# Strided attention: the output products as eight full-array matmuls with a block matrix of weights, the weights turned as 32-bit words, and a store with a nearer wait

## The chip, the cores and the metric

The kernel runs on one core of a Trainium2 chip. Its five engines are TensorE (PE, with PEld for its weight loads), VectorE (DVE), ScalarE (ACT), GpSimd (POOL) and SyncE (SP), which here only issues DMA transfers. The metric is the device time of one execution in microseconds (us). Beside it stands the span of the profiled execution, which is counted from the first to the last event in the trace and is some 1.9 us shorter than that execution's own time.

## The reference

Q, K and V have the shape (8 batches, 12 heads, 1024 positions, 64 dims) in 32-bit floats. Every query attends to 16 keys only, those at positions 0, 64, 128, ... 960:

```python
attend_positions = np.arange(0, seq, stride)          # 16 positions, stride 64
scores = np.einsum('bhqd,bhkd->bhqk', q, k) * scale   # scale = 1/8
weights = np.exp(scores - np.max(scores, axis=-1, keepdims=True))
weights = weights / (np.sum(weights, axis=-1, keepdims=True) + 1e-10)
result[:, :, i, :] = np.einsum('bhqk,bhkd->bhqd', weights, v)[:, :, 0, :]
```

So 96 heads of 1024 x 64 are read and 96 heads of 1024 x 64 are written: 25.2 MB in, 25.2 MB out, and little arithmetic for each byte.

## The kernel before

**Tiling.** The 96 heads are taken as 24 groups (`NG`) of 4 heads. A group is 1 MiB of Q: 128 partitions of 2048 floats. Sixteen groups have a place each in one big buffer, `big`; the outputs of a group overwrite its Q there, and are stored from there. Groups 16 to 23 reuse the first eight places, so their loads wait for the stores of groups 0 to 7.

**One group** runs through these steps, in the names of the code:

1. `cast_a` on ACT and `cast_p` on POOL turn the two halves of Q into bfloat16 (`qb`).
2. `turn` on DVE transposes 32 x 32 blocks of `qb`, as 32-bit words (pairs of bfloat16), into `qt`.
3. `score_products` on PE: scores into PSUM (`sc`).
4. `lay` on DVE transposes the scores into `s_t`; `highest` on DVE takes the maximum over 16 keys (`top`).
5. `subtract` on POOL takes the maximum away (`diff`), `raise_` on ACT takes the exponential (`ex`), `sums` and `inverse` on DVE add up and invert (`total`, `rec`).
6. `normalise` on POOL multiplies `ex` by `rec` into the weights `w_n`, in bfloat16.
7. `back` on DVE transposes `w_n` in 32 x 32 blocks of single bfloat16 values into `w_t`.
8. `output_products` on PE: for each half of the outputs (`h` = 0, 1) eight matmuls, four for each of two 64 x 64 corners of the array, into `o`.
9. `evict` on ACT copies each half from PSUM into `big`.
10. `store` on SP sends the group, or from group 10 on two groups at once (2 MiB), to the output.

`place_k` and `place_v` on POOL bring the keys and values of the next groups into `k_cur` and `v_cur`.

**Order.** The order of the steps is written out by hand. A loop over `n` puts at place n the steps of several groups (`spread(n)`, `turn_over(n + 1)`, `add_up(n - 1)`, `weights_back(n - 2)`, `evict(n - 3, 1)` and so on); each engine runs its own steps in that order. DVE and PE run groups 2 to 21 in hardware loops, `dve_stream` with four groups a round and `pe_stream` with two. SP issues its transfers strictly in order, so a transfer that waits holds up those behind it.

**Waits.** `Program` records every step with what it reads and writes and plans the waits. A step raises either the semaphore of its engine or a named counter, a "gate", which the hardware loops count (`ev` is the gate of evictions; PE waits on it before it overwrites `o`). A step whose signal is a gate cannot be waited for through its engine's semaphore. So where another engine needs such a step, the planner lets it wait for the next step behind it on the same engine that has no gate:

```python
while d is not None and self.ops[d]["gate"]:
    later = (j for j in range(d + 1, i) if self.ops[j]["lane"] == p["lane"])
    d = next(later, None)
```

All evictions carry the gate `ev` except those of the last group, 23. The store of groups 20 and 21 needs the evictions of group 21. The next step on ACT without a gate is the first eviction of group 23, and the store waits for that.

The store of groups 22 and 23, the last, is issued behind a barrier of all engines.

Of the kernel before, what the change touches and what calls it, by code (L numbers as in the profile page):

```python
# [174 lines left out]
def kernel(  # L175
# [38 lines left out]
    s_t = [sb.tile([P, 32, NK], FP32, name=f"s_t{i}") for i in range(2)]  # L214
    diff = [sb.tile([P, 32, NK], FP32, name=f"diff{i}") for i in range(2)]
# [58 lines left out]
    def constants():  # L274
# [14 lines left out]
        for i in range(2):  # L289
            op("DVE", lambda i=i: nc.vector.memset(ex[i], EPS), writes=[f"ex{i}"])  # L290
        op("DVE", lambda: nc.vector.tensor_reduce(
            out=s_sel,
# [73 lines left out]

    def place(to, from_, g, n, needs, writes, gate):
        dims = "pgabx"[: len(to.shape)]
        flat = f"{' '.join(dims)} -> p ({' '.join(dims[1:])})"
        op("POOL", lambda: nc.gpsimd.tensor_copy(  # L370
            out=to[:, g % 2 : g % 2 + n].rearrange(flat).bitcast(I32),
            in_=from_[:, g : g + n].rearrange(flat).bitcast(I32),
        ), reads=needs, writes=writes, gate=None if g == 1 else gate)

    def place_k(g):
        n = 1 if g < 2 else 2
        place(k_cur, k_all, g, n,
              ["k_zero"] + [f"k{i % 2}{s}" for i in range(g, g + n) for s in range(4)],
              [f"k_cur{i % 2}" for i in range(g, g + n)], "stK")

    def place_v(g):
        n = 1 if g < 2 else 2
        place(v_cur, v_all, g, n,
              [f"v_all{i % 2}{x}" for i in range(g, g + n) for x in range(4)],
              [f"v_cur{i % 2}" for i in range(g, g + n)], "stV")

# [18 lines left out]
    def subtract(g):  # L405
        op("POOL", lambda: nc.gpsimd.tensor_tensor(  # L406
            out=diff[g % 2], in0=s_t[g % 2],
            in1=top[g % 2].unsqueeze(2).to_broadcast([P, 32, NK]), op=ALU.subtract,
        ), reads=[f"s_t{g % 2}", f"top{g % 2}"], writes=[f"diff{g % 2}"])

    def raise_(g):
        op("ACT", lambda: nc.scalar.activation(  # L412
            out=ex[g % 2][:, :, 0:NK], in_=diff[g % 2], func=AF.Exp, bias=0.0, scale=scale,
        ), reads=[f"diff{g % 2}"], writes=[f"ex{g % 2}"], gate="ex" if g < LAST - 1 else None)

# [14 lines left out]
    def normalise(g):  # L430
        op("POOL", lambda: nc.gpsimd.tensor_tensor(  # L431
            out=w_n[g % 2], in0=ex[g % 2][:, :, 0:NK],
            in1=rec[g % 2].unsqueeze(2).to_broadcast([P, 32, NK]), op=ALU.mult,
        ), reads=[f"ex{g % 2}", f"rec{g % 2}"], writes=[f"w_n{g % 2}"], gate="wn")

    def back(g):
        return nc.vector.transpose(  # L437
            _ap_with(w_t[g % 2], [w_t[g % 2].ap[0], [64, 8], [1, 2], [2, 32]]),
            w_n[g % 2].rearrange("p n k -> p (n k)"),
        )  # L440

# [8 lines left out]
    def evict(g, h):  # L450
        o = o_ps[h].rearrange("p c (t x d) -> p x (c t) d", t=2, d=D)
        to = big[:, g % NB].rearrange("p (x t d) -> p x t d", x=4, t=8)[:, :, 4 * h : 4 * h + 4]
        op("ACT", lambda: nc.scalar.copy(to, o), reads=[f"o{h}"], writes=[f"b{g % NB}{'ab'[h]}"],  # L453
           gate=None if g == NG - 1 else "ev")

# [37 lines left out]
    def on(f, g, *a, **how):  # L493
        if 0 <= g < NG:
            f(g, *a, **how)
# [53 lines left out]
    def pe_stream(sems, gates):  # L549
# [17 lines left out]
        def output_products(g, h):  # L567
            for t in range(4):
                for b in range(2):
                    half_b = slice(64 * b, 64 * b + 64)  # L570
                    r = pe.matmul(  # L571
                        o_ps[h][half_b, t // 2, 256 * (t % 2) : 256 * (t % 2) + 256],
                        lhsT=w_t[g % 2][half_b, 4 * h + t],
                        rhs=v_cur[half_b, g % 2].rearrange("p x d -> p (x d)"),
                        start=True, stop=True, tile_position=(64 * b, 64 * b),
                    )
            r.then_inc(sems["PE"], 1)
# [88 lines left out]
```

## Time and profile before

| | |
|---|---|
| median of 3 runs | 128.7 us (128.56 to 128.8) |
| profiled execution, own time | 128.46 us |
| its span | 126.6 us |
| busy: PE, DVE, ACT, POOL | 64.2, 100.5, 90.2, 84.2 us |
| DMA: moved, mean rate over the span | 51.15 MB, 404 GB/s |

How to read the views that follow. The page gives busy time of each engine as a share of the span. A stage table gives for each stretch of time the busy microseconds of each engine (with the number of instructions that began there), the granted PE clock as a share of the full one, the mean busy share of the 16 DMA engines and the rate that they moved. A timeline row has the start, the duration, the engine, the line and the operation; merged rows have a count (x16). In square brackets stands how long the engine was idle before, and what ended that. A group row has the count, then the total busy time in us and the mean of one instruction in ns. The chain of waits is the work that ended last, followed back step by step; its rows hold what each step added to the chain, which is less than the duration of an instruction where two overlap.

### The profile page before, as it was taken

Reading aid. Unit: us, or ns where it says so; the run is one execution under the profiler, and the core shown is the slowest. Engines: PE = TensorE matmul, PEld = TensorE weight load, DVE = VectorE, ACT = ScalarE, POOL = GpSimd, SP = SyncE. Lnnn points to the kernel's source line nnn. Section 1 sums busy time; section 2 is a strip of 40 time slices with the busy share of each in tenths; the row PEclk is TensorE's granted clock in tenths of the full one; section 3 lists DMA queues with packets and bytes.
Section 4 is the critical chain, followed back from the end, with each engine's and each line's share of the span. In section 5 each row is a group of like instructions: output and inputs, shape, how many; then the busy total and the mean of one; then the engine's idle time right before and its main releaser. Section 6 shows DMA issues by size and latency. Waiting matters only on the chain.

```text
span 126.6 us, 1871 instructions
## 1 busy us (share of the span) xinstructions
PE 64.2 (51%) x604; PEld 32.7 (26%) x604; DVE 100.5 (79%) x159; ACT 90.2 (71%) x106; POOL 84.2 (67%) x110
## 2 busy tenths in 40 slices
PE   0000702338777788777345777779755336970000
PEld 0000100004543245543112543335522213530000
DVE  4329699499999999999999999999999999520000
ACT  4016679557899988989999789998899669692000
POOL 4016742859888898888898888898888867600000
PEclk9999999999999999999999555555589998699555
DMA  3899999999999989999999989989899999988993
GB/s 93 311 405 441 404 466 445 393 445 404 476 435 393 445 362 422 479 399 396 479 386 430 500 352 453 479 349 494 378 430 430 425 430 425 425 347 342 414 414 166
DMA packets 6803, 51.15 MB, mean 404 GB/s; under 512 B 3760, under 2 KB 3760, under 8 KB 3760
## 3 DMA queue, kind: packets, MB, share of 16 engines
q1 hardware_dynamic: 6800, 51.12, 96.5%
q14 instruction: 3, 0.02, 0.1%
HBM read 25.95 MB, written 25.17 MB: 404 GB/s over the span
## 4 chain that ended last, share of the span: by engine, by line
DVE 68%; ACT 6%; DMA 5%; PE 5%; issue 3%; POOL 3%; DVEq 1%; SPq 0%
DVE qt L361 20%; DVE s_t L392 12%; DVE top L399 11%; DVE total L417 11%; DVE w_t L437 9%; DMA big<-in_K_dram 5%; DVE rec L424 3%; ACT big L453 3%; PE sc L557 2%; PE o L571 2%; DVE v_all L339 2%; POOL qb L357 1%; POOL diff L406 1%; ACT k_all L308 1%; ACT qb L352 1%
## 5 line engine op out<-in xcount | busy, mean ns | idle before, releaser
L453 ACT COPY big<-o 128x1024 f32<-128x1024 f32 x48 | 46.2, 1016 | 8.4 <-PE o L571 8.4
L571 PE MATMUL o<-v_cur,w_t 64*64 64x256 bf16 x384 | 38.5, 361 | 21.1 <-DVE w_t L437 18.6
L571 PEld LDWEIGHTS o<-v_cur,w_t 64*64 64x64 bf16 x384 | 28.7, 142 | 40.5 <-ACT big L453 27.2
L557 PE MATMUL sc<-qt,k_cur 128*32 128x512 bf16 x216 | 25.2, 557 | 15.4 <-DVE qt L361 10.0
L431 POOL TENSOR_TENSOR w_n<-ex,rec 128x512 bf16<-128x512 f32 x24 | 25.4, 1057 | 8.9 <-DVE rec L424 8.9
L406 POOL TENSOR_TENSOR diff<-s_t,top 128x512 f32<-128x512 f32 x24 | 25.4, 1058 | 7.9 <-DVE top L399 7.9
L361 DVE STREAM_TRANSPOSE qt<-qb 128x1024 int32<-128x1024 int32 x24 | 28.8, 1202 | 0.0
L352 ACT CAST qb<-big 128x1024 bf16<-128x1024 f32 x24 | 25.2, 1054 | 0.0
L357 POOL CAST qb<-big 128x1024 bf16<-128x1024 f32 x24 | 25.0, 1043 | 0.0
L412 ACT ACTIVATE ex<-diff 128x512 f32<-128x512 f32 x24 | 15.3, 638 | 6.2 <-POOL diff L406 6.1
L437 DVE STREAM_TRANSPOSE w_t<-w_n 128x512 bf16<-128x512 bf16 x24 | 17.9, 746 | 1.6 <-POOL w_n L431 1.5
L392 DVE STREAM_TRANSPOSE s_t<-sc 128x512 f32<-128x512 f32 x24 | 16.1, 671 | 1.6 <-PE sc L557 1.6
L417 DVE TENSOR_REDUCE total<-ex 128x32 f32<-128x544 f32 x24 | 17.0, 707 | 0.3 <-ACT ex L412 0.3
L399 DVE TENSOR_REDUCE top<-s_t 128x32 f32<-128x512 f32 x24 | 15.5, 647 | 0.1
L557 PEld LDWEIGHTS sc<-qt,k_cur 128*32 128x32 bf16 x216 | 3.6, 103 | 26.9 <-DVE qt L361 19.8
L315 PE MATMUL o<-big,perm_v 128*128 128x384 bf16 x4 | 1.5, 520 | 12.8 <-POOL big L323 12.8
L424 DVE RECIPROCAL rec<-total 128x32 f32<-128x32 f32 x24 | 7.4, 308 | 0.0
L370 POOL COPY v_cur<-v_all 128x256 int32<-128x256 int32 (+1 forms) x13 | 5.0, 384 | 1.1 <-PE o L571 1.1
L370 POOL COPY k_cur<-k_all 128x128 int32<-128x128 int32 (+1 forms) x13 | 3.7, 281 | 2.1 <-ACT k_all L308 1.8
L298 ACT CAST big<-big 128x384 bf16<-128x384 f32 x1 | 0.5, 511 | 5.6 <-DMA big<-in_K_dram 5.6
L299 POOL CAST big<-big 128x384 bf16<-128x384 f32 x1 | 0.5, 507 | 5.6 <-DMA big<-in_K_dram 5.6
L301 DVE STREAM_TRANSPOSE big<-big 128x384 int32<-128x384 int32 x1 | 0.6, 579 | 4.3 <-POOL big L299 4.3
(18 smaller groups left out, 18.8 us busy)
## 6 DMA issues: line engine op xcount, KB each, us to landing
big<-in_Q_dram SPq DMA_DIRECT2D x24, 1024.0 KB, 12.2
out_dram<-big SPq DMA_DIRECT2D x7, 2048.0 KB, 13.7
out_dram<-big SPq DMA_DIRECT2D x10, 1024.0 KB, 14.1
big<-in_K_dram SPq DMA_DIRECT2D x1, 384.0 KB, 6.8
big<-in_V_dram SPq DMA_DIRECT2D x1, 384.0 KB, 7.9
```

The lines of the kernel that those rows point to most:

```text
L352: op("ACT", lambda: nc.scalar.copy(b[:, half:], q[:, half:]), reads=[f"b{g % NB}{h}" for h in "ab"], writes=[f"qb{g % 4}1"])
L357: op("POOL", lambda: nc.gpsimd.tensor_copy(out=b[:, 0:half], in_=q[:, 0:half]), reads=[f"b{g % NB}{h}" for h in "ab"] + [f"qb{g % 4}1"] * ...
L361: return nc.vector.transpose(qt[g % 2].bitcast(I32), qb[g % 4].bitcast(I32))
L392: return nc.vector.transpose(s_t[g % 2].rearrange("p n k -> p (n k)"), sc_ps[g % 2])
L399: return nc.vector.tensor_reduce(out=top[g % 2], in_=s_t[g % 2], op=ALU.max, axis=mybir.AxisListType.X)
L406: op("POOL", lambda: nc.gpsimd.tensor_tensor(out=diff[g % 2], in0=s_t[g % 2], in1=top[g % 2].unsqueeze(2).to_broadcast([P, 32, NK]), op=AL ...
L417: return nc.vector.tensor_reduce(out=total[g % 2], in_=ex[g % 2], op=ALU.add, axis=mybir.AxisListType.X)
L431: op("POOL", lambda: nc.gpsimd.tensor_tensor(out=w_n[g % 2], in0=ex[g % 2][:, :, 0:NK], in1=rec[g % 2].unsqueeze(2).to_broadcast([P, 32, N ...
L437: return nc.vector.transpose(_ap_with(w_t[g % 2], [w_t[g % 2].ap[0], [64, 8], [1, 2], [2, 32]]), w_n[g % 2].rearrange("p n k -> p (n k)"),)
L453: op("ACT", lambda: nc.scalar.copy(to, o), reads=[f"o{h}"], writes=[f"b{g % NB}{'ab'[h]}"], gate=None if g == NG - 1 else "ev")
L557: r = pe.matmul(sc_ps[g % 2][32 * c : 32 * c + 32], lhsT=k_cur[:, g % 2, f, b], rhs=_ap_with(qt[g % 2], [qt[g % 2].ap[0], [D, 8], [16 * D, ...
L571: r = pe.matmul(o_ps[h][half_b, t // 2, 256 * (t % 2) : 256 * (t % 2) + 256], lhsT=w_t[g % 2][half_b, 4 * h + t], rhs=v_cur[half_b, g % 2] ...
```

## The change

The weights of a group are now laid out and turned in another way, and the output products are made from a block matrix:

- `normalise` writes `w_n` with two bytes of every four: the weights of two neighbouring groups of queries (x = 0, 1) alternate, so that a pair lies in one 32-bit word. Its reads are as before.
- `back` transposes `w_n` as 32-bit words, in two instructions for 64 partitions each, into the two diagonal 64 x 64 blocks of `w_t`, which is now 128 wide. The other two blocks are set to zero once, by two new `memset` instructions at the start on DVE.
- `output_products` makes four matmuls of 128 x 128 by 256 columns for each half where it made eight of 64 x 64 by 256.
- `subtract` works in place in `s_t`; the tile `diff` is gone, and `raise_` reads `s_t`.
- The second eviction of group 21 has no gate any more. A step that does nothing but wait for it on ACT raises the gate `ev` in its stead. The store of groups 20 and 21 thereby waits for this eviction itself.
- `place_k` and `place_v` are written out separately, and do the same.

```diff
-    w_t = [sb.tile([P, 8, 64], BF16, name=f"w_t{i}") for i in range(2)]
+    w_t = [sb.tile([P, 8, P], BF16, name=f"w_t{i}") for i in range(2)]
...
+        for i in range(2):
+            op("DVE", lambda i=i: nc.vector.memset(w_t[i], 0.0), writes=[f"w_t{i}"])
...
     def subtract(g):
         op("POOL", lambda: nc.gpsimd.tensor_tensor(
-            out=diff[g % 2], in0=s_t[g % 2],
+            out=s_t[g % 2], in0=s_t[g % 2],
             in1=top[g % 2].unsqueeze(2).to_broadcast([P, 32, NK]), op=ALU.subtract,
-        ), reads=[f"s_t{g % 2}", f"top{g % 2}"], writes=[f"diff{g % 2}"])
+        ), reads=[f"s_t{g % 2}", f"top{g % 2}"], writes=[f"s_t{g % 2}"])
...
     def normalise(g):
         op("POOL", lambda: nc.gpsimd.tensor_tensor(
-            out=w_n[g % 2], in0=ex[g % 2][:, :, 0:NK],
-            in1=rec[g % 2].unsqueeze(2).to_broadcast([P, 32, NK]), op=ALU.mult,
+            out=_ap_with(w_n[g % 2], [w_n[g % 2].ap[0], [64, 8], [1, 2], [32, 2], [2, NK]]),
+            in0=ex[g % 2][:, :, 0:NK].rearrange("p (t x u) k -> p t x u k", x=2, u=2),
+            in1=rec[g % 2].rearrange("p (t x u) -> p t x u", x=2, u=2).unsqueeze(4).to_broadcast([P, 8, 2, 2, NK]),
+            op=ALU.mult,
         ), reads=[f"ex{g % 2}", f"rec{g % 2}"], writes=[f"w_n{g % 2}"], gate="wn")
 
     def back(g):
-        return nc.vector.transpose(
-            _ap_with(w_t[g % 2], [w_t[g % 2].ap[0], [64, 8], [1, 2], [2, 32]]),
-            w_n[g % 2].rearrange("p n k -> p (n k)"),
-        )
+        for b in range(2):
+            rows = slice(64 * b, 64 * b + 64)
+            r = nc.vector.transpose(
+                w_t[g % 2][rows, :, rows].bitcast(I32),
+                w_n[g % 2][rows].rearrange("p n k -> p (n k)").bitcast(I32),
+            )
+        return r
...
         op("ACT", lambda: nc.scalar.copy(to, o), reads=[f"o{h}"], writes=[f"b{g % NB}{'ab'[h]}"],
-           gate=None if g == NG - 1 else "ev")
+           gate=None if g == NG - 1 or (g, h) == (NG - 3, 1) else "ev")
...
         on(evict, n - 3, 1)
+        if n - 3 == NG - 3:
+            op("ACT", lambda: nc.scalar.nop(), reads=[f"b{(NG - 3) % NB}b"], gate="ev")
...
         def output_products(g, h):
             for t in range(4):
-                for b in range(2):
-                    half_b = slice(64 * b, 64 * b + 64)
-                    r = pe.matmul(
-                        o_ps[h][half_b, t // 2, 256 * (t % 2) : 256 * (t % 2) + 256],
-                        lhsT=w_t[g % 2][half_b, 4 * h + t],
-                        rhs=v_cur[half_b, g % 2].rearrange("p x d -> p (x d)"),
-                        start=True, stop=True, tile_position=(64 * b, 64 * b),
-                    )
+                r = pe.matmul(
+                    o_ps[h][:, t // 2, 256 * (t % 2) : 256 * (t % 2) + 256],
+                    lhsT=w_t[g % 2][:, 4 * h + t],
+                    rhs=v_cur[:, g % 2].rearrange("p x d -> p (x d)"),
+                    start=True, stop=True,
+                )
             r.then_inc(sems["PE"], 1)
```

Where this shows in the order of the instructions: first DVE, one group in the hardware loop, before. A row holds the line, the operation, what it writes and reads (the number behind a name tells two buffers apart) and the size of its output.

```order
L392 STREAM_TRANSPOSE s_t_73<-sc_92 128x512
L361 STREAM_TRANSPOSE qt_72<-qb_70 128x1024
L399 TENSOR_REDUCE top_83<-s_t_73 128x32
L417 TENSOR_REDUCE total_86<-ex_78 128x32
L437 STREAM_TRANSPOSE w_t_81<-w_n_79 128x8x2x32
L424 RECIPROCAL rec_88<-total_86 128x32
```

The same place now:

```order
L389 STREAM_TRANSPOSE s_t_73<-sc_90 128x512
L362 STREAM_TRANSPOSE qt_72<-qb_70 128x1024
L396 TENSOR_REDUCE top_81<-s_t_73 128x32
L414 TENSOR_REDUCE total_84<-ex_76 128x32
L438 STREAM_TRANSPOSE w_t_79<-w_n_77 64x8x32 x2
L421 RECIPROCAL rec_86<-total_84 128x32
```

One transpose of 512 elements a partition has become two, of 256 32-bit words a partition each, at the same place.

Next the end of ACT's program, with the semaphores each instruction waits for, before. The rows are the exponential of group 22, both evictions of group 20, the exponential of group 23, both evictions of group 21 and the first of group 22.

```order
L412 ACTIVATE ex0_77<-diff0_75 128x32x16 [waits at_POOL]
L453 COPY big_66<-o0_94 128x4x256 [waits at_PE]
L453 COPY big_66<-o1_95 128x4x256 [waits at_PE]
L412 ACTIVATE ex1_78<-diff1_76 128x32x16 [waits at_POOL]
L453 COPY big_66<-o0_94 128x4x256 [waits at_PE]
L453 COPY big_66<-o1_95 128x4x256 [waits at_PE]
L453 COPY big_66<-o0_94 128x4x256 [waits at_PE]
```

And now:

```order
L409 ACTIVATE ex0_75<-s_t0_73 128x32x16 [waits at_POOL]
L455 COPY big_66<-o0_92 128x4x256 [waits at_PE]
L455 COPY big_66<-o1_93 128x4x256 [waits at_PE]
L409 ACTIVATE ex1_76<-s_t1_74 128x32x16 [waits at_POOL]
L455 COPY big_66<-o0_92 128x4x256 [waits at_PE]
L455 COPY big_66<-o1_93 128x4x256 [waits at_PE]
L455 COPY big_66<-o0_92 128x4x256 [waits at_ACT,at_PE]
```

The instructions are the same; ahead of the first eviction of group 22 (the last row) stands the new wait of ACT for its own eviction of group 21. SP's transfers stand in the same order as before.

More of the change, by code (lines that the diff above doesn't have):

```diff
@@ L406, in subtract @@
         op("POOL", lambda: nc.gpsimd.tensor_tensor(
[L407 removed]
+            out=s_t[g % 2], in0=s_t[g % 2],
             in1=top[g % 2].unsqueeze(2).to_broadcast([P, 32, NK]), op=ALU.subtract,
[L409 removed]
+        ), reads=[f"s_t{g % 2}", f"top{g % 2}"], writes=[f"s_t{g % 2}"])
     def raise_(g):
         op("ACT", lambda: nc.scalar.activation(
[L413 to L414 removed]
+            out=ex[g % 2][:, :, 0:NK], in_=s_t[g % 2], func=AF.Exp, bias=0.0, scale=scale,
+        ), reads=[f"s_t{g % 2}"], writes=[f"ex{g % 2}"], gate="ex" if g < LAST - 1 else None)
     def sums(g):
```

24 lines of the change are left out of this document (10 added, 14 removed).

## Prediction

> **What bounds the kernel now.** I read the page first, for the busy shares and the chain.
>
> ```profile
> span 126.6 us, 1871 instructions
> PE 64.2 (51%) x604; PEld 32.7 (26%) x604; DVE 100.5 (79%) x159; ACT 90.2 (71%) x106; POOL 84.2 (67%) x110
> q1 hardware_dynamic: 6800, 51.12, 96.5%
> DVE 68%; ACT 6%; DMA 5%; PE 5%; issue 3%; POOL 3%; DVEq 1%; SPq 0%
> ```
>
> The chain of waits says DVE. The queue of the transfers says something else: its 16 engines were taken for 96.5% of the span. Both can be nearly full, so the question is which of them the end waits for. The stage table answers that; its last two columns are the DMA share and the rate in GB/s.
>
> ```profile
> 26.00:41.00 15.00, 10.48 (x88) 5.62 (x90) 15.00 (x25) 11.75 (x14) 12.08 (x16) 1.00 1.00 430
> 86.00:101.00 15.00, 9.11 (x101) 4.96 (x99) 15.00 (x25) 13.05 (x16) 13.35 (x17) 0.77 1.02 431
> 113.00:113.60 0.60, 0.51 (x8) 0.24 (x6) 0.00 (x0) 0.60 (x1) 0.00 (x0) 1.00 0.65 273
> 113.60:114.80 1.20, 0.00 (x0) 0.00 (x0) 0.00 (x0) 1.07 (x2) 0.00 (x0) 1.00 0.07 27
> 114.80:124.60 9.80, 0.00 (x0) 0.00 (x0) 0.00 (x0) 0.00 (x0) 0.00 (x0) 0.60 1.01 428
> 124.60:126.60 2.00, 0.00 (x0) 0.00 (x0) 0.00 (x0) 0.00 (x0) 0.00 (x0) 0.50 0.00 0
> ```
>
> In the loop DVE is busy for 15.00 of 15 us, and the transfers run at 430 GB/s with a share of 1.0, early and late. The rate is the same 428 GB/s at the end, where no engine works any more. So I take 428 GB/s as what the transfers can do here, and DVE as an engine that merely keeps up: it makes outputs while a backlog of transfers stands ahead of them. The backlog runs out once: from 113.60 to 114.80 the transfers stand still (27 GB/s). Then 4 MiB are left, which take the 9.80 us to 124.60; 2.00 us of closing follow. Why they stand still is seen on the timeline.
>
> ```profile
> 104.92 0.54 SPq L34 DMA_DIRECT2D out_dram<-big  x1
> 108.71 1.93 ACT L453 COPY big<-o 128x1024 f32<-128x1024 f32 x2 [1.02 <-PE o L571]
> 110.91 3.76 ACT L453 COPY big<-o 128x1024 f32<-128x1024 f32 x4 [0.27 <-PE o L571]
> 113.78 0.54 SPq L34 DMA_DIRECT2D out_dram<-big  x1
> 115.04 0.54 SPq L34 DMA_DIRECT2D out_dram<-big  x1
> SPq L34 <- ACT big L453: 8.3, 1, 8.3
> ```
>
> The three transfers are the stores of groups 18+19, 20+21 and 22+23. Group 21 is evicted by 108.71 + 1.93 = 110.64. Its store goes out at 113.78, just after the third of the next four evictions (110.91 + 3 x 0.94 = 113.73), the first of group 23. Its data move from 114.80, 1.0 us after the issue. By then the store of groups 18+19 has been through for 1.2 us.
>
> **The store's wait.** With its wait on the eviction that it needs, the store of groups 20+21 goes out at about 110.7, and could move data from 111.7. The store ahead holds the transfers until 113.6. So there is no gap: the remaining 4 MiB run from 113.6 to 113.6 + 9.8 = 123.4, provided that the last store is there in time. It is issued at 115.04 and could move from 116.0; the store ahead of it needs until 113.6 + 4.9 = 118.5. The gain is the stall of 1.20 us, less the 27/428 of it (0.08 us) that did move something. The slow 0.6 us before it (273 GB/s) may give (1 - 273/428) x 0.6 = 0.22 us more, as a queue that does not run dry has no tailing off. That is **1.1 to 1.35 us, taken as 1.2**. The new step on ACT waits only for ACT's own eviction; behind it stand the evictions of groups 22 and 23. The first of these began 0.27 us after the one before it anyway, for want of PE: this covers the step. If it took more, the last store would be late by the difference, and has 2.5 us to spare.
>
> **The turn on DVE.** The chain's rows give what each step of a group adds, overlap left out:
>
> ```profile
> 58.45 0.66 DVE w_t L437
> 59.12 0.21 DVE rec L424
> 59.32 0.58 DVE s_t L392
> 59.90 1.12 DVE qt L361
> 61.02 0.57 DVE top L399
> 61.59 0.62 DVE total L417
> ```
>
> Together 3.76 us a group. Two transposes of 256 words replace one of 512 values (0.66). No 64-partition transpose is in the trace. From 512 elements (0.58, `s_t`) to 1024 words (1.12, `qt`) an element costs 1.05 ns, and 0.04 us is left as fixed cost: 256 words then take 0.31, two of them 0.62, **0.04 us less** than now. The other end comes from the shortest DVE step, the reciprocal: 32 elements take 0.21, so up to 0.18 us could be fixed. Then two halves take 2 x (0.27 + 0.18) = 0.90, 0.24 us more. I take 0.62, since it comes from the same operation; nothing speaks for less, as both forms pass 512 elements. Over 24 groups that is 1.0 us earlier on DVE, and worth nothing: the transfers are full without it, and the earlier stores would only stand in the queue longer.
>
> **The margin.** How late may the evictions become? The store of groups 20+21 could move from 111.7 and is wanted at 113.6: 1.9 us. Beyond that each microsecond late is one lost, and the gain is gone at 1.9 + 1.2 = 3.1 us. Spread over groups 0 to 21 that is 0.14 us a group, from whichever engine.
>
> **The strided write on POOL.**
>
> ```profile
> L431 POOL TENSOR_TENSOR w_n<-ex,rec 128x512 bf16<-128x512 f32 x24 | 25.4, 1057 | 8.9 <-DVE rec L424 8.9
> L406 POOL TENSOR_TENSOR diff<-s_t,top 128x512 f32<-128x512 f32 x24 | 25.4, 1058 | 7.9 <-DVE top L399 7.9
> L357 POOL CAST qb<-big 128x1024 bf16<-128x1024 f32 x24 | 25.0, 1043 | 0.0
> L370 POOL COPY v_cur<-v_all 128x256 int32<-128x256 int32 x11 | 4.4, 400 | 1.1 <-PE o L571 1.1
> ```
>
> `normalise` and `subtract` take the same 1057 and 1058 ns, though one writes 2 bytes an element and the other 4: the size of the write sets nothing here. No row writes every other 2 bytes. One more pass of the data through POOL would be the upper bound: the one-input rows (1043 for 1024, 400 for 256) give 0.84 ns an element, so 512 elements 0.43 us. POOL is busy for 13.35 of 15 us, so of a group's 3.76 us 0.41 is free. Hence 0 to 0.43 us is taken in, to 0.02 us a group; I take 0, by the two equal rows. `subtract` in place moves as many bytes as before: 0.
>
> The Trainium skill ("GPSIMD Engine Reference", section 7, Performance pitfalls) has a rule that could speak against this: reads whose inner step is over 8 bytes cost about half as much again. It tells of reads; here the new step is 4 bytes and on a write, and the read of `ex` keeps its step. By that rule the sum stays as it is. No row of this trace has such a step on POOL.
>
> **The matmuls.**
>
> ```profile
> 59.22 1.06 PE L571 MATMUL o<-v_cur,w_t 64*64 64x256 bf16 x16 [0.86 <-DVE w_t L437]
> 55.41 1.91 PE L571 MATMUL o<-v_cur,w_t 64*64 64x256 bf16 x16 [0.90 <-DVE w_t L437]
> 12.82 1.46 PE L315 MATMUL o<-big,perm_v 128*128 128x384 bf16 x4 [12.82 <-POOL big L323]
> 59.27 0.64 ACT L412 ACTIVATE ex<-diff 128x512 f32<-128x512 f32 x1
> 61.51 0.70 DVE L417 TENSOR_REDUCE total<-ex 128x32 f32<-128x544 f32 x1
> ```
>
> A group's sixteen 64 x 64 matmuls take 1.06 us, or 1.91 in slow stretches. The only full-array matmuls are four of 384 columns at the start, 1.46 us; eight of 256 columns scale to 1.46 x 2 x 256/384 = 1.95 us as an upper bound, and half of the slow row (0.5 us) is below anything seen. I take the same as now. The ends stay harmless: PE is idle for 30% of the loop or more (10.48 and 9.11 of 15 us are busy), and at worst a group's outputs come 0.9 us later. ACT then evicts later, and its exponential behind that: it ends at 59.91 where DVE wants it at 61.51, 1.6 us to spare. Behind the loop, where PE itself is on the chain, 0.9 us a group for two groups stays below the 1.9 us of margin.
>
> **The two memsets** stand on DVE ahead of the first reduction.
>
> ```profile
> 3.28 1.08 DVE L290 MEMSET ex<- 128x544 f32 x2
> 4.29 0.23 DVE L291 TENSOR_REDUCE s_sel<-identity 128x4 f32<-128x128 bf16 x1
> 8.81 0.58 DVE L301 STREAM_TRANSPOSE big<-big 128x384 int32<-128x384 int32 x1 [4.30 <-POOL big L299]
> ```
>
> Two like them take 1.08 us, and DVE waits 4.30 us there for the keys. Without that cover they would cost those 1.08 us, within the margin.
>
> **The sum** is -1.2 us, all from the store's wait: 128.46 - 1.2 = 127.26 us by the profiled execution, whose own time is 0.24 us below the median shown. Moved to the median it is 127.5. **I predict 127.4 us**; with the 1.1 to 1.35 and the spread of the runs shown, 127.0 to 127.8 is this case's own range.
>
> **The rivals.**
>
> The forecast: the stall goes, all else is covered. 0.73.
>
> More: if 428 GB/s were what the stores happen to offer and not a limit, DVE's 1.0 us would come on top, and the time would be 126.4 us. Against it: the rate is the same with and without work beside it. 0.04.
>
> The stall moves instead of going. Two stores then drain together, and the transfers could fall back to the 273 GB/s seen before the stall at the joint between two stores, or the last store may wait for something late in the barrier ahead of it (its issue at 115.04 already comes 0.37 after the last eviction's end at 114.67). Then the time stays within 0.2% of now (about what runs of this kernel can tell from no change): 128.5 to 128.9 us. Against it speaks that every earlier store follows another without a dip to be seen in the stage rows. 0.09.
>
> Slower, by DVE. If a transpose of 64 partitions pays the reciprocal's fixed cost, a group takes 4.00 us in place of 3.76. DVE is busy without pause, so it all adds up: 22 x 0.24 = 5.3 us at group 21. The store of groups 20+21 then moves from 111.7 + 5.3 = 117.0, and its data and the last end at 126.8, 2.2 us later than the 124.6 now: 130.7 us. It decides from 0.14 us a group, that is, from 0.40 us a half. For it: no row shows this form. Against it: all long steps fit 0.04 us fixed, and the reciprocal may be slow by itself. 0.08.
>
> Slower, by POOL. If the strided write doubles `normalise` to 2.11 us, POOL has 1.06 - 0.41 = 0.65 us a group too little, 14.3 us over 22 groups: data end at 111.7 + 14.3 + 9.8 = 135.8, and the time is 139.7 us. It decides from 0.41 + 0.14 = 0.55 us an instruction, above the extra pass of 0.43. At half as much again (0.53) it is 128.0 us. 0.04 for the slow case, 0.02 for the one between.
>
> **How the numbers follow.** Faster by over 0.2%: the forecast, the case of more and POOL's case between, 0.73 + 0.04 + 0.02 = 0.79. Within it: 0.09. Slower: 0.08 + 0.04 = 0.12. The range from 126.6 to 128.5 holds the forecast, POOL's middle case, half of the case of more and the edge of the no-change case, about 0.8.
>
> **What would show it.** In the changed profile: the store of groups 20+21 issued within 0.2 us of the second eviction of group 21, and no stage between 104 and 122 us with a DMA share far below 1.0; `w_t` at two rows of about 0.31 in the chain; `normalise` at 1.06 us; the span near 125.4. DVE's loop should close some 0.9 us earlier with nothing gained by it. I am wrong if the transfers are not the limit: if an end of DVE 1 us earlier moves the end by as much, or if 428 GB/s is exceeded over a long stretch. I am wrong on the other side if `w_t` or `w_n` is longer than the bounds above.

## The result, and the profile after

| | before | after |
|---|---|---|
| median | 128.62 us (128.52 to 128.8, 5 runs) | 130.78 us (130.63 to 130.97, 5 runs) |
| ratio | | 1.0168, 95% interval 1.0154 to 1.0182 |
| profiled execution, span | 128.46, 126.6 us | 130.88, 129.0 us |
| one group on DVE, in the chain | 3.76 us | 4.07 us |
| second eviction of group 21 ends | 110.64 us | 116.39 us |

The change makes the kernel 2.2 us slower. One run of all is left out of the figures: 160.91 us for the changed kernel with the old wait, whose other three runs took 134.24 to 134.39. First the page of the changed kernel: busy shares and the queue.

```profile
span 129.0 us, 1514 instructions
PE 66.9 (52%) x412; PEld 26.4 (20%) x412; DVE 107.5 (83%) x185; ACT 90.3 (70%) x106; POOL 84.2 (65%) x110
q1 hardware_dynamic: 6800, 51.12, 94.7%
```

DVE is busy 7.0 us longer than before (100.5), and the queue's share has gone down from 96.5 to 94.7%: transfers now wait for something. The chain of waits of the changed kernel shows for what; start, time added and work in each row, one group:

```profile
60.56 0.34 DVE w_t L438
60.90 0.01 issue
60.92 0.44 DVE w_t L438
61.36 0.03 issue
61.39 0.35 DVE rec L421
61.74 0.57 DVE s_t L389
```

From the start of the first half of the turn to the start of `s_t` it is 61.74 - 60.56 = 1.18 us, where turn and reciprocal took 59.32 - 58.45 = 0.87 us before. The 0.31 us are the whole difference between 4.07 and 3.76 us a group. Two things strike: the second half adds 0.44 us, 0.10 more than the first of the same size, and the reciprocal behind it adds 0.35 + 0.03 us, where it added 0.21.

The timeline of the changed kernel at the end:

```profile
110.57 0.54 SPq L34 DMA_DIRECT2D out_dram<-big  x1
114.46 1.93 ACT L455 COPY big<-o 128x1024 f32<-128x1024 f32 x2 [0.82 <-PE o L573]
116.41 0.54 SPq L34 DMA_DIRECT2D out_dram<-big  x1
118.94 1.93 ACT L455 COPY big<-o 128x1024 f32<-128x1024 f32 x2 [0.17 <-PE o L573]
121.04 0.54 SPq L34 DMA_DIRECT2D out_dram<-big  x1
```

The store of groups 20+21 goes out 0.02 us after the eviction that it needs (114.46 + 1.93 = 116.39), as the change intends. But this eviction comes 5.75 us later than before. The stage table of the changed kernel (again the DMA share and GB/s in the last two columns):

```profile
109.60:110.80 1.20, 0.53 (x5) 0.52 (x6) 1.16 (x4) 0.63 (x1) 0.45 (x2) 1.00 0.00 0
117.00:117.60 0.60, 0.60 (x11) 0.12 (x8) 0.33 (x1) 0.60 (x1) 0.24 (x1) 1.00 0.00 0
117.60:118.20 0.60, 0.21 (x4) 0.00 (x0) 0.55 (x2) 0.60 (x2) 0.00 (x0) 1.00 1.01 437
122.20:122.80 0.60, 0.00 (x0) 0.00 (x0) 0.00 (x0) 0.00 (x0) 0.00 (x0) 1.00 1.03 437
127.60:129.00 1.40, 0.00 (x0) 0.00 (x0) 0.00 (x0) 0.00 (x0) 0.00 (x0) 0.50 0.00 0
```

Now the transfers do stand still, at 0 GB/s, ahead of the store of groups 18+19 and ahead of that of 20+21. The last 4 MiB start at 117.6, 1.2 us after the issue (116.41), and run at the full share from there on. Their last packet ends at 127.5 (125.05 in the kernel before), 1.5 us ahead of the end of the span.

The other parts of the change, first in the groups of the changed kernel (count, busy us, mean ns):

```profile
L428 POOL TENSOR_TENSOR w_n<-ex,rec 128x512 bf16<-128x512 f32 x24 | 25.5, 1061 | 15.9 <-DVE rec L421 15.9
L438 DVE STREAM_TRANSPOSE w_t<-w_n 64x256 int32<-64x256 int32 x48 | 20.9, 435 | 1.9 <-POOL w_n L428 1.6
```

and then on its timeline:

```profile
110.27 1.03 PE L573 MATMUL o<-v_cur,w_t 128*128 128x256 bf16 x8 [0.99 <-issue]
113.41 1.86 PE L573 MATMUL o<-v_cur,w_t 128*128 128x256 bf16 x8
4.42 1.03 DVE L291 MEMSET w_t<- 128x512 uint32 x2
8.59 0.58 DVE L302 STREAM_TRANSPOSE big<-big 128x384 int32<-128x384 int32 x1 [2.85 <-POOL big L300]
```

The strided write costs nothing (1061 ns against 1057), eight full matmuls take what sixteen small ones took (1.03 and 1.86 us against 1.06 and 1.91), and the memsets lie where DVE still has 2.85 us to wait. So two questions are left: what in the two halves costs 0.31 us a group, and where the 1.2 us of the store's wait are.

### The profile page after: what moved, and what is told of

The parts are those of the page before. It is cut to its first block, busy times and chain, and to the rows that moved or that the text cites. A ratio compares the mean times of both kernels' runs of the same rounds, so it can differ in the third digit from the quotient of the medians.

```text
span 129.0 us, 1514 instructions
## 1 busy us (share of the span) xinstructions
PE 66.9 (52%) x412; PEld 26.4 (20%) x412; DVE 107.5 (83%) x185; ACT 90.3 (70%) x106; POOL 84.2 (65%) x110
## 3 DMA queue, kind: packets, MB, share of 16 engines
q1 hardware_dynamic: 6800, 51.12, 94.7%
## 4 chain that ended last, share of the span: by engine, by line
DVE 70%; DMA 6%; PE 4%; issue 4%; POOL 3%; ACT 2%; SPq 2%; DVEq 1%; ACTq 1%; POOLq 0%
DVE qt L362 20%; DVE s_t L389 11%; DVE w_t L438 11%; DVE top L396 11%; DVE total L414 11%; DMA big<-in_V_dram 6%; DVE rec L421 6%; PE o L573 2%; DVE v_all L340 2%; PE sc L561 1%; SPq L34 1%; POOL w_n L428 1%; POOL s_t L403 1%; ACT big L455 1%; ACT qb L353 1%
## 5 line engine op out<-in xcount | busy, mean ns | idle before, releaser
L573 PE MATMUL o<-v_cur,w_t 128*128 128x256 bf16 x192 | 39.1, 371 | 22.8 <-DVE w_t L438 20.8
L428 POOL TENSOR_TENSOR w_n<-ex,rec 128x512 bf16<-128x512 f32 x24 | 25.5, 1061 | 15.9 <-DVE rec L421 15.9
L561 PE MATMUL sc<-qt,k_cur 128*32 128x512 bf16 x216 | 26.6, 584 | 17.1 <-DVE qt L362 10.6
L573 PEld LDWEIGHTS o<-v_cur,w_t 128*128 128x128 bf16 x192 | 22.3, 125 | 49.6 <-issue 39.8
L403 POOL TENSOR_TENSOR s_t<-s_t,top 128x512 f32<-128x512 f32 x24 | 25.4, 1058 | 7.1 <-DVE top L396 7.1
L438 DVE STREAM_TRANSPOSE w_t<-w_n 64x256 int32<-64x256 int32 x48 | 20.9, 435 | 1.9 <-POOL w_n L428 1.6
L409 ACT ACTIVATE ex<-s_t 128x512 f32<-128x512 f32 x24 | 15.3, 638 | 6.8 <-POOL s_t L403 6.8
L421 DVE RECIPROCAL rec<-total 128x32 f32<-128x32 f32 x24 | 8.5, 353 | 0.7
L309 DVE COPY k_all<-big 32x384 bf16<-32x384 bf16 x6 | 3.5, 588 | 0.1
```

Of the source, the lines that this page charges most:

```text
L403: op("POOL", lambda: nc.gpsimd.tensor_tensor(out=s_t[g % 2], in0=s_t[g % 2], in1=top[g % 2].unsqueeze(2).to_broadcast([P, 32, NK]), op=ALU ...
L428: op("POOL", lambda: nc.gpsimd.tensor_tensor(out=_ap_with(w_n[g % 2], [w_n[g % 2].ap[0], [64, 8], [1, 2], [32, 2], [2, NK]]), in0=ex[g % 2 ...
L438: r = nc.vector.transpose(w_t[g % 2][rows, :, rows].bitcast(I32), w_n[g % 2][rows].rearrange("p n k -> p (n k)").bitcast(I32),)
L561: r = pe.matmul(sc_ps[g % 2][32 * c : 32 * c + 32], lhsT=k_cur[:, g % 2, f, b], rhs=_ap_with(qt[g % 2], [qt[g % 2].ap[0], [D, 8], [16 * D, ...
L573: r = pe.matmul(o_ps[h][:, t // 2, 256 * (t % 2) : 256 * (t % 2) + 256], lhsT=w_t[g % 2][:, 4 * h + t], rhs=v_cur[:, g % 2].rearrange("p x ...
```

## The experiments

### The turn: one instruction, or two

**One turn.** All of the change, but the weights are turned in one instruction of 128 partitions into a compact `w_t`, and the matmuls stay the sixteen of 64 x 64.

```diff
     def back(g):
-        for b in range(2):
-            rows = slice(64 * b, 64 * b + 64)
-            r = nc.vector.transpose(
-                w_t[g % 2][rows, :, rows].bitcast(I32),
-                w_n[g % 2][rows].rearrange("p n k -> p (n k)").bitcast(I32),
-            )
-        return r
+        return nc.vector.transpose(
+            w_t[g % 2].rearrange("p t m -> p (t m)").bitcast(I32),
+            w_n[g % 2].rearrange("p n k -> p (n k)").bitcast(I32),
+        )
```

> The whole change, but the weights are turned as 32-bit words by one transpose of 128 partitions into a compact matrix of 64 columns, and the sixteen 64 x 64 matmuls are kept (so no block matrix and no memsets). Theory that the split into two instructions of 64 partitions is what costs: the one turn adds 0.31 us to DVE's chain in place of 0.66 before and 0.83 in the changed kernel, the reciprocal behind it adds 0.21 again in place of 0.35, and the time is that of the transfers, 127.3 to 127.5 us. Rival, that turning words or the strided weights cost by themselves: a turn of 0.5 us or more and a group on DVE of 3.76 us or more. Rival, that the transfers are no limit: DVE's gain of some 2 us shows and the time is below 126.5 us.

Measured: 128.54 us (10 runs), ratio 0.9997 (0.9986 to 1.0008). The chain of waits of this kernel:

```profile
59.90 0.35 DVE w_t L434
60.25 0.23 DVE rec L419
60.49 0.58 DVE s_t L387
...
63.37 0.35 DVE w_t L434
```

A turn of 256 words adds 0.35 us whether it has 128 or 64 partitions, and a group takes 3.47 us, less than the 3.76 of before. The loss is in the two halves. And DVE, faster by 0.29 us a group, brings nothing against before.

**The halves in other order.** Partitions 64 to 127 first, then 0 to 63.

```diff
-        for b in range(2):
+        for b in (1, 0):
```

> The changed kernel with the two halves of the turn in the other order, partitions 64 to 127 first. Theory that an instruction which begins at partition 64 pays, or makes the next one pay: the first half now adds about 0.45 us and the second 0.36, and the reciprocal is back at about 0.21. Rival, that the second of two short instructions pays, wherever it begins: steps as in the changed kernel, 0.36, 0.47 and 0.35, and the same 130.8 us.

Measured: 130.65 us (1 run). The chain of waits:

```profile
60.44 0.03 issue
60.47 0.44 DVE w_t L438
60.91 0.01 issue
60.92 0.44 DVE w_t L438
61.36 0.23 DVE rec L421
```

The total is the same, but its parts have moved: now the first half is as long as the second, 0.44 us, and the reciprocal is back at 0.23.

**Both halves on the same partitions.** Both instructions read and write partitions 0 to 63. The lower 64 partitions are not turned, so half of the outputs is left out; the work of every engine is otherwise the same in kind and amount.

```diff
-                w_t[g % 2][rows, :, rows].bitcast(I32),
-                w_n[g % 2][rows].rearrange("p n k -> p (n k)").bitcast(I32),
+                w_t[g % 2][0:64, :, rows].bitcast(I32),
+                w_n[g % 2][0:64].rearrange("p n k -> p (n k)").bitcast(I32),
```

> The changed kernel with both halves of the turn on partitions 0 to 63: the second reads the same weights again and writes them beside the first, so the weights of partitions 64 to 127 stay zero and half of the output is left out. Two instructions of the same size, but none begins at partition 64. Theory that an instruction whose partitions begin in another place than those of the one before is held until that one has finished: nothing is held now, start to start 0.36 and 0.36 for the halves and 0.23 for the reciprocal, 3.83 us a group in place of 4.07, and the last evictions about 5 us earlier: 128.4 to 128.8 us, as the kernel before. Rival, that two short instructions cost by themselves: 0.45, 0.45 and 0.27, and 130.8 us.

Measured: 128.15 us (127.94 to 128.3, 5 runs), ratio 0.9958 (0.9945 to 0.9971). The chain of waits:

```profile
62.22 0.68 DVE w_t L438 x2
62.90 0.23 DVE rec L421
63.13 0.57 DVE s_t L389
...
66.02 0.68 DVE w_t L438 x2
```

**One turn, split along the words.** Two instructions of 128 partitions with 128 words each, in the kernel with one turn.

```diff
-        return nc.vector.transpose(
-            w_t[g % 2].rearrange("p t m -> p (t m)").bitcast(I32),
-            w_n[g % 2].rearrange("p n k -> p (n k)").bitcast(I32),
-        )
+        for t in (0, 4):
+            r = nc.vector.transpose(
+                w_t[g % 2][:, t : t + 4].rearrange("p t m -> p (t m)").bitcast(I32),
+                w_n[g % 2][:, 4 * t : 4 * t + 16].rearrange("p n k -> p (n k)").bitcast(I32),
+            )
+        return r
```

> The one turn of 128 partitions (compact weights, 64 x 64 matmuls, nearer wait) split along the words: two instructions of 128 partitions and 128 words each. It measures the fixed cost of a turn alone. From 0.36 us for 256 words start to start and 1.04 ns a word, 0.09 us is fixed: two of 128 words take 0.45 us, then 0.23 for the reciprocal. Rival, a floor on short instructions: 0.6 us or more for the two. The time is 128.5 us in both cases, as the transfers set it.

Measured: 128.46 us (1 run). The chain of waits:

```profile
60.38 0.41 DVE w_t L435 x2
60.79 0.23 DVE rec L419
```

**What follows.** A second instruction as such costs 0.06 us (0.41 against 0.35), and two halves of 64 partitions take 0.68 us if they start on the same partition. What makes the changed kernel slow is that its instructions start on different partitions. Where one starts on the same partition as the one before it, it begins 0.07 to 0.08 us before that one ends; where it starts elsewhere, it begins 0.01 to 0.03 us after that end, so the two do not overlap. That is so in the traces for the first half behind the reduction (order 64, 0) and for the second half behind the first, which add 0.44 where a half added 0.34, and for the reciprocal, which adds 0.35 + 0.03 where it added 0.23. In the order 0, 64, reciprocal at 0, the second half and the reciprocal are hit; in the order 64, 0, reciprocal at 0, the two halves. That is what the two chains show, row by row.

The Trainium skill has this as a rule ("VectorE: DVE Perf Modes", section "Two Vector instructions with no wait between them"): an instruction whose input or output starts in another group of 32 partitions than the last one read or written is held until every earlier one has finished. All four traces agree with it: it names the held instructions in both orders, and none in the kernels with one turn or with both halves on partition 0. The page gives no size; here it is 0.11 us for a half and 0.15 us for the reciprocal (0.38 against 0.23).

### The store: the wait alone, and the wait left out

**The store alone.** The kernel before, with the two edits of the store's wait and nothing else.

```diff
-           gate=None if g == NG - 1 else "ev")
+           gate=None if g == NG - 1 or (g, h) == (NG - 3, 1) else "ev")
...
+        if n - 3 == NG - 3:
+            op("ACT", lambda: nc.scalar.nop(), reads=[f"b{(NG - 3) % NB}b"], gate="ev")
```

> The kernel before with the nearer wait of the store of groups 20+21 alone (its eviction without a gate, the waiting step on ACT). Theory: the transfers stand still for 1.2 us from 113.6 to 114.8 in the kernel before, and this gap closes: 127.3 to 127.5 us, no stage between 104 and 122 us with a low DMA share. Rival: the stall moves to another joint between two stores, 128.5 to 128.9 us.

Measured: 128.69 us (10 runs), ratio 1.0004 (0.9995 to 1.0014): nothing. The timeline of this kernel, and then its stage table:

```profile
107.75 1.93 ACT L453 COPY big<-o 128x1024 f32<-128x1024 f32 x2 [0.33 <-PE o L573]
109.70 0.54 SPq L34 DMA_DIRECT2D out_dram<-big  x1
```

```profile
113.60:114.80 1.20, 0.00 (x0) 0.00 (x0) 0.00 (x0) 0.37 (x1) 0.00 (x0) 0.62 1.00 423
114.80:122.80 8.00, 0.00 (x0) 0.00 (x0) 0.00 (x0) 0.00 (x0) 0.00 (x0) 0.50 1.01 428
122.80:123.40 0.60, 0.00 (x0) 0.00 (x0) 0.00 (x0) 0.00 (x0) 0.00 (x0) 0.50 0.33 137
123.40:124.00 0.60, 0.00 (x0) 0.00 (x0) 0.00 (x0) 0.00 (x0) 0.00 (x0) 0.50 0.07 27
124.00:124.60 0.60, 0.00 (x0) 0.00 (x0) 0.00 (x0) 0.00 (x0) 0.00 (x0) 0.50 0.06 27
```

The wait does all that was foreseen: the store goes out 0.02 us after its eviction, the gap is filled, and most of the data are through by 123.3. But then 27 GB/s go on until 124.6, just where the data ended before. And 27 GB/s is one sixteenth of 430: one of the 16 DMA engines, alone. The 1.2 us have moved from 113.6 to 123.4.

Each transfer is shared by 16 engines, and each of these reports when its share has landed. From those reports, worked out for the last five stores of 2 MiB (groups 14+15 to 22+23): the median of the 16, the last, and the lag between them, in us.

```
                 median    last     lag
before           104.46   105.41   0.95
                 109.37   110.54   1.18
                 114.26   115.70   1.44
                 120.42   120.67   0.25
                 125.27   125.49   0.23
store alone      104.08   105.50   1.41
                 108.98   110.73   1.75
                 113.89   115.77   1.88
                 118.80   120.63   1.84
                 123.70   125.58   1.88
```

In both kernels one engine lags, by 0.13 to 0.34 us more with each store of 2 MiB; with the store alone it stays at 1.8 to 1.9 us from the third of these stores on. In the kernel before, the gap at 113.6 is where the other 15 wait for data and the late one works off its backlog: behind it the lag is 0.25. So the end gains nothing from a gap closed, as the late engine had none: the median report comes 1.57 us earlier (125.27 to 123.70), and the last one at 125.58 instead of 125.49.

**The old wait in the kernel with one turn.** The kernel with one turn, but the store waits as before.

```diff
-           gate=None if g == NG - 1 or (g, h) == (NG - 3, 1) else "ev")
+           gate=None if g == NG - 1 else "ev")
...
-        if n - 3 == NG - 3:
-            op("ACT", lambda: nc.scalar.nop(), reads=[f"b{(NG - 3) % NB}b"], gate="ev")
```

> The one turn of 128 partitions as before, but with the old wait of the store of groups 20+21. Evictions end about 5 us earlier than in the kernel before, so even the old wait is over before the transfers run dry. Theory that one of the 16 DMA engines is behind the others and never stands still, and that its work sets the end: 128.4 to 128.7 us with and without the nearer wait, and near the end 15 engines finish about 1.8 us before the last. Rival, that closing the gap by itself is what costs elsewhere: below 128.2 us.

Measured: 128.52 us (10 runs), ratio 0.9994 (0.9982 to 1.0005). In this run two engines are late: their last reports come at 125.08 and 125.42, those of the other 14 by 123.98. Neither a DVE that is 0.29 us a group faster nor the store's wait changes the time, alone or together: in all of these the late engines set it.

**The changed kernel with the old wait.** The same edit in the changed kernel.

> The changed kernel with the old wait of the store of groups 20+21 (all else of the change as it is). Theory: that store then goes out only after the first eviction of group 23, at about 120.0 us, and 4 MiB are left to move from 121.0 on: data end near 130.8, span 132.8, time 134.6 us, so the nearer wait is worth 3.8 us in the slowed kernel. Rival, that the last store alone sets the end: 130.8 us as the changed kernel.

Measured: 134.38 us (134.24 to 134.39, 3 runs), ratio 1.0446 (1.0422 to 1.0469). The stage table:

```profile
117.00:120.60 3.60, 1.73 (x18) 0.83 (x16) 0.88 (x2) 3.05 (x4) 0.13 (x1) 1.00 0.00 0
122.20:130.60 8.40, 0.00 (x0) 0.00 (x0) 0.00 (x0) 0.00 (x0) 0.00 (x0) 0.50 1.03 437
```

Here the transfers wait at 0 GB/s, all 16 engines, for 3.6 us and more. The nearer wait is worth 134.38 - 130.78 = 3.6 us once the evictions are late, and nothing while they are not.

### Which engine is late

These four change only the last store of the kernel with one turn (128.54 us). What tells them apart is how many engines take a piece of it. The Trainium skill ("DMA: Bandwidth & Descriptors", section "Why a DMA increments its semaphore by 16 and not by 1") states that a transfer uses the largest number up to 16 that divides the slowest dimension of both sides, and for queues like SP's the lowest-numbered engines. No row here shows an engine's number, so "the low eight" below rests on that page. How many engines take a piece, the reports do show: with the data come 15 and 8 for the pieces of 120 and 8 partitions, and 8, 7, 8 and 16 for the arrays of 8 x 16, 7 x 16, 8 x 14 and 16 x 7 rows.

**In 120 and 8 partitions.**

```diff
-    end = send(NG - 2, 2)
+    for p0, rows in ((0, 120), (120, 8)):
+        end = send(NG - 2, 2, p0, rows)
```

> The one turn of 128 partitions with the nearer wait, and the last store (groups 22+23) as two transfers, of 120 partitions and of 8, in place of one of 128. If a transfer is spread over as many of the 16 engines as divide its partitions, the first is left to 15 engines and the second to 8, so one engine gets none of the last 2 MiB and eight get an eighth more. Theory that one engine, some 1.8 us behind, sets the end: if it is the one left out, the others' end of about 123.4 plus 0.6 for the eight decides, and the time is 127.3 to 127.6 us; if it is one of the eight, 129.1 us; if one of the other seven, 128.5. Rival, that the end is set by the total rate: 128.5 to 129.1 us, never faster.

Measured: 131.54 us (131.24 to 131.62, 4 runs), ratio 1.0218 (1.0201 to 1.0235). The stage table:

```profile
121.00:124.00 3.00, 0.00 (x0) 0.00 (x0) 0.00 (x0) 0.00 (x0) 0.00 (x0) 0.50 0.88 257
124.00:126.00 2.00, 0.00 (x0) 0.00 (x0) 0.00 (x0) 0.00 (x0) 0.00 (x0) 0.50 0.46 147
```

At a share of 0.88 the engines move 257 GB/s, where 1.01 was 428 before: the packets themselves are slower. A packet of 16 KB takes 0.62 us in the loop of this run (median, 100 to 110 us) and 0.91 to 1.07 us from 122 to 125. The time therefore says nothing on the late engine; this one is inconclusive.

**A quarter of it as 8 x 16 rows.**

```diff
-    end = send(NG - 2, 2)
-    tc.declare_no_dep(end.ins, landed, reason="waits for the older stores alone")
+    o = big[:, (NG - 2) % NB : (NG - 2) % NB + 2]
+    at, run = (NG - 2) * HG * SD, 16 * D
+    parts = [
+        (_ap_with(out, [[run, P], [2 * SD, 3], [1, run]], at), _ap_with(o, [o.ap[0], [1, 1], [1, 3 * run]])),
+        (_ap_with(out, [[16 * run, 8], [run, 16], [1, run]], at + 6 * SD),
+         _ap_with(o, [o.ap[0], [1, 1], [1, run]], 3 * run)),
+    ]
+    for to, from_ in parts:
+        end = _copy(nc, to, from_)
+        tc.declare_no_dep(end.ins, landed, reason="waits for the older stores alone")
```

> The one turn of 128 partitions with the nearer wait; the last store as two transfers: three quarters of each partition's 16 KB over all 16 engines as ever, and the last quarter (0.5 MiB) written as eight times sixteen rows, which is meant for eight engines. An engine works off 16 KB in 0.61 us, so the eight get two pieces' worth of work more than in the even split (1.2 us), and the other eight two less. Fifteen engines end at 123.3 in the even split, one at 125.2. If the late engine is among the eight that are spared: end at 124.5, time 127.8 us, faster than the kernel before. If it is among the eight that carry more: end at 126.4, 129.7 us. Rival, that the total rate sets the end: 123.5 + 1.2 = 124.7, 128.0 us in either case, with no engine late. If the transfer is spread over 16 engines after all: 128.5 us.

Measured: 129.84 us (10 runs), ratio 1.0076 (1.0055 to 1.0098). The last engine reports at 126.86 us, 1.18 us later than with the plain store (125.68). That report is one of the eight of the array; the other seven come by 125.32.

**336 KiB of it as 7 x 16, 8 x 14 and 16 x 7 rows.** Three kernels with the same four pieces; only the array of the third piece differs. The cut below is the one with 7 x 16 rows, against the kernel with 8 x 16.

```diff
-        (_ap_with(out, [[16 * run, 8], [run, 16], [1, run]], at + 6 * SD),
-         _ap_with(o, [o.ap[0], [1, 1], [1, run]], 3 * run)),
+        (_ap_with(out, [[run, P], [1, 1], [1, 256]], at + 6 * SD), _ap_with(o, [o.ap[0], [1, 1], [1, 256]], 3 * run)),
+        (_ap_with(out, [[16 * run, 7], [run, 16], [1, 768]], at + 6 * SD + 256),
+         _ap_with(o, [[o.ap[0][0], 112], [1, 1], [1, 768]], 3 * run + 256)),
+        (_ap_with(out, [[run, 16], [1, 1], [1, 768]], at + 6 * SD + 112 * run + 256),
+         _ap_with(o, [[o.ap[0][0], 16], [1, 1], [1, 768]], 112 * o.ap[0][0] + 3 * run + 256)),
```

> The kernel with one turn and the nearer wait; of the last store's 2 MiB, 336 KiB (the last 3 KiB of 112 partitions) go out as an array of 7 x 16 rows, meant for the seven lowest DMA engines, so these carry 27 KiB more than a sixteenth (1.0 us by 16 KiB in 0.61 us) and the other nine 21 KiB less (0.8 us). Theory A, the late engine is number 7, the one of the low eight that is not among the seven: it ends 0.8 us earlier and the seven, which were done by 123.3, end at 124.3: 127.7 to 127.9 us against 128.5 with the plain last store. Theory B, the late engine is among the seven: 128.5 + 1.0 = 129.5 us. Theory C, no engine in particular, the lag goes to whichever ends last: 128.1 to 128.9 us.

> The same pieces, but the 336 KiB go out as 8 x 14 rows, meant for the eight lowest DMA engines: these carry 21 KiB more than a sixteenth (0.8 us), the other eight 21 KiB less. Theories A and B both have the late engine among the eight: 128.5 + 0.8 = 129.3 us, so that under A one row of the array more or less (7 or 8) changes the time by 1.5 us. Theory C: 128.1 to 128.9 us, as with seven.

> The control for the arrays of 7 x 16 and 8 x 14 rows (129.66 and 129.63 us): the same four pieces of the last store with the same rows, but the 336 KiB go out as 16 x 7 rows, over all 16 DMA engines, so that no engine carries more than a sixteenth. If the extra 1.1 us of those two is the load of the low engines, the time is that of the plain last store, 128.4 to 128.7 us, and the late engine ends at its 124.6 to 125.2. If it is the price of a store in pieces, whichever engines carry them, the time is 129.3 to 129.7 us, and which engine is late stays open.

| rows | median | ratio to before | last engine reports |
|---|---|---|---|
| 7 x 16 | 129.66 us (6 runs) | 1.0075 (1.0057 to 1.0092) | 126.81 us |
| 8 x 14 | 129.63 us (6 runs) | 1.0065 (1.0046 to 1.0083) | 126.72 us |
| 16 x 7 | 128.77 us (11 runs) | 1.0008 (0.9999 to 1.0017) | 125.79 us |

The stage tables near the end, of 7 x 16 and then of 16 x 7 rows:

```profile
125.40:126.00 0.60, 0.00 (x0) 0.00 (x0) 0.00 (x0) 0.00 (x0) 0.00 (x0) 0.50 0.13 51
```

```profile
124.60:125.20 0.60, 0.00 (x0) 0.00 (x0) 0.00 (x0) 0.00 (x0) 0.00 (x0) 0.50 0.06 26
125.20:126.90 1.70, 0.00 (x0) 0.00 (x0) 0.00 (x0) 0.00 (x0) 0.00 (x0) 0.50 0.00 0
```

The pieces themselves cost 0.2 us at most (16 x 7: 1.0008, 0.9999 to 1.0017). With more work on seven or eight engines the end comes 0.9 us later still, so the late engine is among those that got more, the seven included. The reports show it too. Of the eight of the array of 8 x 14 rows the last comes at 126.54, the others by 124.85. Of the seven of the array of 7 x 16 rows five come by 124.97 and two at 126.42 and 126.62: in that run two engines were late (51 GB/s are two engines' worth), and both are among the seven. The control with 16 x 7 rows ran on another chip than these two; each ratio is to the kernel before on the same chip. The Trainium skill ("DMA: Bandwidth & Descriptors", section "Latency and other measured facts") calls engines 7 and 15 usually slower than the rest in traces, with a best guess at the cause that applies to another kind of queue only. The engines that are late here are neither of them, if the seven are those that its rule names. As by that rule a piece can only choose the lowest engines, none of these arrays spares the late one, and no complete kernel of this study was faster than before.

## Why the prediction was wrong, point by point

**What bounds the kernel.** "428 GB/s as what the transfers can do here, and DVE as an engine that merely keeps up" held: DVE at 3.47 in place of 3.76 us a group gains nothing (0.9997). The case of more, 126.4 us, is thereby out. What this reading left out is that the 16 engines need not end together: where the end is set by the transfers, the latest engine sets it and not the rate of all.

**The store's wait: the step that failed on the gain.** "The transfers stand still (27 GB/s)" misread the row. They did not stand still; one engine of 16 worked there at its full rate, and it is this one that ends last. The term took the gap as lost time for all 16 engines. The store went out as computed, and the rate was kept through the gap as computed, but the gap was no loss to the late engine. The term of -1.2 us measured +0.1 (ratio 1.0004, 0.9995 to 1.0014). "The stall moves instead of going" with 128.5 to 128.9 us was the right case for this part. Its reasons were not: neither a joint between two stores nor the barrier was it.

**The turn: the step that failed on the loss.** 0.62 us was the term for both halves. Two halves that are not held take 0.68. The rest is what no term stood for: 0.11 us because the second half is held, and about 0.15 for the held reciprocal, so that the edit adds 0.31 us a group where -0.04 was taken. The upper bound of 0.90 for the turn did hold (0.34 + 0.01 + 0.44 = 0.79), but the instruction behind the turn was outside of the bound. Without the holds the forecast that nothing is lost would have stood: with both halves on one partition a group takes 66.02 - 62.22 = 3.80 us, the 0.04 us more are 0.9 us over 22 groups, within the margin of 1.9, and the time is 128.15 us.

**The rival "slower, by DVE"** gave 130.7 us, and 130.78 was measured, but the reason that it gave, a larger fixed cost, is not what costs here. The fixed cost is small, 0.35 - 256 x 0.00105 = 0.08 us for the turn of 256 words, twice the 0.04 taken and far from the 0.18 of the bound. That 0.24 us a group was close to the true 0.31 is luck. So is 22 x 0.24 = 5.3 us for the lateness of group 21, against 5.75 measured: 22 x 0.31 would be 6.8. In the chains four groups, one round of the hardware loop, take 57.68 - 41.40 = 16.28 us from one `s_t` to the next where they took 55.42 - 40.29 = 15.13. That is 1.15 us a round and not 4 x 0.31, as the first group of a round took 44.19 - 40.29 = 3.90 us already before; five rounds make the 5.75.

**The margin** was right, and is what makes the time come out. The eviction of group 21 is 116.39 - 110.64 = 5.75 us late; less the margin of 1.9 and the gap's 1.2 the end should be 2.65 us later, and the span grew by 2.4. The start of the last data was foreseen at 117.0 for that case and lies at 117.6. All 16 engines start there together, behind a stretch of 0 GB/s, so no engine has a backlog (the 16 reports of the last store come from 127.77 to 127.94), and the sum holds without a term for a late one. With the old wait, the 3.6 us more follow in the same way.

**POOL, matmuls, memsets** were right: 0, the same, and hidden, by the rows above. One reading was not: PE is idle for less than 30% in two other stages of the loop, where it is busy for 11.49 (41 to 56 us) and 11.51 (71 to 86 us) of 15 us, that is, idle for 23%. Nothing came of it.

## What to carry to other kernels

A stretch at one sixteenth of the full rate need not be a stall: here one DMA engine still worked, and what feeds the other fifteen sooner gains nothing if that one ends last. So take the time of a transfer from the last of its engines, not from the rate. On VectorE, splitting an instruction over partitions cost more than its fixed cost: count every instruction that starts on other partitions than the one before it (0 and 64 here), the short one behind the pair included, and split along the free dimension where that can be chosen (0.41 us here, against 0.79).

## What the runs showed of the hardware

- (VectorE) A turn that starts on other partitions than the one before it adds 0.44 us instead of 0.34, and a reciprocal of 32 elements added 0.38 us instead of 0.23.
- In the kernel before and in that with the store's wait alone, one DMA engine lags behind the others by 0.13 to 0.34 us more with every 2 MiB stored; at 1.8 to 1.9 us the lag stops growing. In other runs two engines lag (7 x 16 rows, the old wait in the kernel with one turn, both halves on the same partitions). Behind a stretch in which all 16 wait, the lag is gone (0.1 us in the changed kernel). Why an engine lags, and why the lag stops, stays open.
- A store in 120 and 8 partitions instead of 128 slowed the packets around it: 257 GB/s at a share of 0.88. Which of the two pieces does it was not tried.
- The kernel with both halves on the same partitions is 0.4% faster than before (0.9945 to 0.9971), although one DVE group of it is 0.04 us longer. Its lag at the end is 1.75 us, of two engines. Why it gains is not settled; half of its outputs are left out of the turn.
